# Moving the rows of the normalised input to another place in SBUF

## The chip, the cores and the metric

The kernel runs on one core of a Trainium2 chip. A core has a matrix engine (TensorE, PE in the profile, its weight loads PEld), a vector engine (VectorE, DVE), a scalar engine (ScalarE, ACT), GpSimd (POOL) and SyncE (SP), which issues transfers. On-chip memory (SBUF) has 128 partitions; a tile has a start address in bytes, the same in every partition, and rows of so many bytes. The metric is device time in microseconds for one execution.

## The reference

One layer of a hybrid decoder over 512 tokens with 16 learned meta tokens in front, 1024 channels, float32. What matters here is that one normalised input `u` is multiplied by the many columns of one wide weight matrix:

```python
u = rmsnorm(h, mix_norm_w[i])
proj = u @ w_in[i]                      # (528, 1024) @ (1024, 9248)
u_pool = proj[..., OFF_POOL:OFF_Z]      # all 528 tokens needed
z = proj[..., OFF_Z:OFF_XBC]            # tokens behind the meta tokens
xbc = proj[..., OFF_XBC:OFF_DT]         # all 528
gates = jax.nn.sigmoid(proj[..., OFF_GATE:] + b_gate[i])   # behind the meta tokens
...
y_pool = pool_mixer(u_pool, ...) @ w_pool_up[i]
y_ssd = mamba2_branch(z, xbc, ...) @ w_ssd_out[i]
h = h + (gate_pool * y_pool + gate_ssd * y_ssd) @ w_o[i]
v = rmsnorm(h, mlp_norm_w[i])
h = h + jnp.square(jax.nn.relu(v @ w_ff1[i])) @ w_ff2[i]
out = rmsnorm(h, final_norm_w)          # meta tokens dropped
```

## The kernel before

Every matmul is done in three: a float32 operand is split into a high and a low part of type float32r (ScalarE makes the high part, VectorE the rest), and high by high, high by low and low by high are summed in PSUM. The weights come in blocks of 128 x 1024, loaded by SyncE in the order of use and split into `whi` and `wlo` (lines 68 to 70).

The input lies transposed, channels on the partitions: eight tiles `k` of 128 channels, each with a row of 528 numbers (16 meta tokens, then 512). `xh`, `xl` are the input split, used while the norm is not yet known; `uh`, `ul` (line 119 on) are the normalised input, split. `norm_u` writes them once, about 70 us from the start; all further products with `w_in` read them.

`proj` (line 138 to 141 is its inner step) multiplies one weight block by all eight `k`. For each `k` it issues weights high by `uh[k]`, weights high by `ul[k]`, and weights low by `uh[k]`; the weights are the stationary operand, the rows of `uh`, `ul` the moving one. There are two uses:

- `narrow`: the 512 tokens behind the meta tokens in one matmul: `pz` (in `group_proj`, two blocks to a group), `pgp` and `pgs` (gates).
- `wide`: all tokens in two pieces of 264 columns, or 258 where the first 12 are skipped: `px` (projections to `x`, `B`, `C` of the state space branch) and `pp` (pooling branch).

The work on `uh`, `ul` is woven with that of the state space branch (`ssd`, up to about 510 us): `weave` takes turns between the parts of one group's `ssd` and the projections of the next. After it come the pooling branch with `pool_tile` and `pool_mix` (`pp`, `pg`), `w_pool_up` (`pup`) and the second gates (`pgs`) until 646 us. Then the output projection (`pw`), and the MLP (`pf`, `alpha`, `p2`, `q5`, last the products at line 849). Those do not read `uh`, `ul`; their moving operands are `mh`, `vh`, `vl`, `whi`, `wlo` and the like. `mm3` (lines 86 to 88) issues their three matmuls in the same order as `proj`.

Tiles are laid out by pools: a pool on the left side begins where the pools opened before it end, its tiles one after the other in the order in which they are asked for, each start a multiple of 32 bytes. At address 0 lies a scratch of 16384 bytes for the descriptors of GpSimd's transfers. Of the addresses that the kernel before has:

| tiles | start | modulo 256 |
|---|---|---|
| `raw`, `whi`, `wlo` | 23008 and on, 4096 each | 224 |
| `uh0` to `uh7`, `ul0` to `ul7` | 68064 and on, 2112 each | 224, 32, 96, 160 and again |
| the tokens behind the meta tokens, 64 bytes on | | 32, 96, 160, 224 and again |
| `vh`, `vl`, `mh`, `ml`, `yph`, `ypl`, `yh`, `yl`, `ph`, `pl` | 2048 each | 224 |
| the float32 tiles of `ssd` (pool `gs`), `qhg`, `qlg` among them | 122720 and on | 96 |

The left side of SBUF and the right side meet with little room: in `ssd` the left pools end at 160608 and the right ones begin at 163808; in the pooling branch they end at 128736 and begin at 131040.

Of the kernel before, what the change touches and what calls it, by code (L numbers as in the profile page):

```python
# [9 lines left out]
F32 = mybir.dt.float32  # L10
F32R = mybir.dt.float32r
# [3 lines left out]
P = 128  # L15
D = 1024
SEQ = 512
NM = 16
L = SEQ + NM
HALF = L // 2  # L20
NK = D // P
# [24 lines left out]
def kernel(ctx: ExitStack, tc, xT, x, w, vec, fnw, out):  # L46
    nc = tc.nc
# [68 lines left out]

    u_stack = ExitStack()
    up = u_stack.enter_context(tc.tile_pool(name="up", bufs=1, side="left"))
    uh = [up.tile([P, L], F32R, name=f"uh{k}") for k in range(NK)]
    ul = [up.tile([P, L], F32R, name=f"ul{k}") for k in range(NK)]  # L120

    gc_stack = ExitStack()
    gc = gc_stack.enter_context(tc.tile_pool(name="gc", bufs=2, side="left", reuse_waits="tile"))
# [503 lines left out]
    for half in range(2):  # L627
# [5 lines left out]
        for kk in range(4):  # L633
            wh, wl = block()
            for k2 in range(2):
                k = 2 * kk + k2
# [8 lines left out]
        for kk in range(4):  # L645
            k = 4 * half + kk
# [185 lines left out]
    for t in range(4):  # L832
        T, st = t // 2, slice((t % 2) * P, (t % 2 + 1) * P)
        n = 0
        for half in range(2):
            parts = [(0, 512)] if half == 0 or t < 3 else [(0, 256), (256, 256)]
            for a, m in parts:
# [4 lines left out]
                for k, seg in ((1, (A11, 3)[T]), (0, (A12, A22)[T])):  # L842
                    wh, wl = wq[k, half]
                    for p in range(2):
                        x0 = p * 512 + a
                        f = i == 0 and not (T == 0 and half == 0)
# [151 lines left out]
```

## Time and profile before

| | us |
|---|---|
| median of 3 runs | 1035.13 (1034.96 to 1035.14) |
| the profiled execution | 1035.26 |
| its span, first to last instruction | 1033.5 |

| matmuls by moving operand | columns | count |
|---|---|---|
| `pz`, `pgp`, `pgs` from `uh`, `ul` | 512 | 336, 120, 192 |
| `px` from `uh`, `ul` | 264 | 1008 |
| `px` from `uh`, `ul` | 258 | 336 |
| `pp` from `uh`, `ul` | 264 | 384 |
| all matmul instructions | | 5700 |

A profile is of one execution. It has for every engine the start and the duration of each instruction and what released it. Matmuls overlap: a row's mean duration is longer than the distance from one start to the next, which is the pace of the stream. The span is some 1.8 us shorter than the time of the same execution.

### The profile page before, as it was taken

What the parts mean: (1) busy time and instruction counts of PE and PEld (TensorE: products, weight loads), DVE (VectorE), ACT (ScalarE), POOL (GpSimd) and SP (SyncE); (2) the same over time, 40 slices, a digit from 0 to 9 for tenths busy, and PEclk for the clock granted to TensorE, in tenths of its full rate; (3) what the DMA queues carried; (4) which work ended last, traced back from release to release, by engine and by line L of the source; (5) the groups of instructions that cost most, each with busy time, mean ns of one, the idle gap of its engine ahead of it and who ended that gap; (6) DMA issues with size and microseconds to landing.
All of it is one profiled execution on the core that took longest, in us unless ns stands there. A gap on an engine that the chain in (4) does not pass through costs nothing.

```text
span 1033.5 us, 13995 instructions
## 1 busy us (share of the span) xinstructions
PE 1019.6 (99%) x5700; PEld 880.2 (85%) x5700; DVE 714.2 (69%) x932; ACT 542.3 (52%) x706; POOL 9.9 (1%) x24
## 2 busy tenths in 40 slices
PE   7999999999999999999999999999999999999997
PEld 7889988898879898988998888878888888888886
DVE  7978787687636586878664345645686676776866
ACT  7675968586627349573443123344555354454444
POOL 0100000000000000000000000000000000000000
PEclk9999999999999999999999999999999999999999
DMA  6343041414332321413232323533324323334112
GB/s 229 110 140 103 21 164 37 148 47 137 102 112 73 103 101 41 146 59 111 77 107 95 102 81 102 204 126 122 99 82 123 103 81 122 102 102 123 42 41 82
DMA packets 29424, 106.01 MB, mean 103 GB/s; under 512 B 3312, under 2 KB 4272, under 8 KB 28336
## 3 DMA queue, kind: packets, MB, share of 16 engines
q1 hardware_dynamic: 26640, 93.14, 28.8%
q0 software_dynamic: 2000, 11.08, 2.9%
q8 instruction: 45, 0.74, 0.3%
q10 hardware_dynamic: 720, 0.91, 0.3%
q14 instruction: 19, 0.16, 0.0%
HBM read 102.95 MB, written 2.16 MB: 102 GB/s over the span
## 4 chain that ended last, share of the span: by engine, by line
PE 97%; DVE 1%; DMA 1%; ACT 0%; issue 0%; SPq 0%; ACTq 0%
PE px L138 6%; PE px L141 6%; PE px L139 6%; PE pf L86 6%; PE pf L87 6%; PE pf L88 6%; PE alpha L742 3%; PE alpha L743 3%; PE alpha L744 3%; PE pz L139 3%; PE pz L141 3%; PE pz L138 3%; PE py L416 2%; PE pso L86 2%; PE pp L141 2%; PE pp L139 2%
## 5 line engine op out<-in xcount | busy, mean ns | idle before, releaser
L69 ACT CAST whi<-raw 128x1024 fp32r<-128x1024 f32 (+2 forms) x141 | 145.4, 1037 | 274.3 <-PE pf L87 61.3
L70 DVE TENSOR_TENSOR wlo<-raw,whi 128x1024 fp32r<-128x1024 f32 (+2 forms) x141 | 169.8, 1206 | 151.5 <-ACT whi L69 151.5
L138 PE MATMUL px<-uh,whi 128*128 128x264 f32 (+1 forms) x448 | 121.0, 291 | 0.7 <-DVE ct L280 0.7
L139 PE MATMUL px<-ul,whi 128*128 128x264 f32 (+1 forms) x448 | 118.2, 284 | 0.0
L86 PE MATMUL pf<-vh,whi 128*128 128x512 f32 x256 | 99.7, 389 | 1.2 <-DVE vl L651 1.2
L87 PE MATMUL pf<-vl,whi 128*128 128x512 f32 x256 | 99.6, 389 | 0.0
L88 PE MATMUL pf<-vh,wlo 128*128 128x512 f32 x256 | 99.6, 389 | 0.0
L141 PE MATMUL px<-uh,wlo 128*128 128x264 f32 (+1 forms) x448 | 91.5, 285 | 0.0
L138 PEld LDWEIGHTS px<-uh,whi 128*128 128x128 f32 x448 | 84.6, 189 | 2.8 <-issue 2.6
L139 PEld LDWEIGHTS px<-ul,whi 128*128 128x128 f32 x448 | 84.4, 188 | 0.3
L141 PEld LDWEIGHTS px<-uh,wlo 128*128 128x128 f32 x448 | 69.4, 188 | 0.3 <-issue 0.3
L693 DVE TENSOR_TENSOR slo<-b,shi 128x1024 fp32r<-128x1024 f32 x35 | 42.7, 1220 | 31.6 <-ACT shi L692 31.6
L692 ACT CAST shi<-b 128x1024 fp32r<-128x1024 f32 x35 | 36.7, 1050 | 51.9 <-PE pf L87 36.5
L86 PEld LDWEIGHTS pf<-vh,whi 128*128 128x128 f32 x256 | 48.1, 188 | 11.5 <-DVE vl L651 1.5
L88 PEld LDWEIGHTS pf<-vh,wlo 128*128 128x128 f32 x256 | 48.0, 188 | 10.0
L87 PEld LDWEIGHTS pf<-vl,whi 128*128 128x128 f32 x256 | 48.1, 188 | 9.8
L742 PE MATMUL alpha<-shi,hh 128*128 128x512 f32 x140 | 54.6, 390 | 0.0
L743 PE MATMUL alpha<-slo,hh 128*128 128x512 f32 x140 | 54.5, 389 | 0.0
L744 PE MATMUL alpha<-shi,hl 128*128 128x512 f32 x140 | 54.5, 389 | 0.0
L754 DVE TENSOR_TENSOR ht<-ht,alpha 128x1024 f32<-128x1024 f32 x35 | 42.6, 1216 | 6.1 <-PE alpha L744 6.1
L139 PE MATMUL pz<-ul,whi 128*128 128x512 f32 x112 | 44.3, 395 | 0.0
L141 PE MATMUL pz<-uh,wlo 128*128 128x512 f32 x112 | 44.1, 394 | 0.0
(330 smaller groups left out, 2395.8 us busy)
## 6 DMA issues: line engine op xcount, KB each, us to landing
raw<-in_w SPq DMA_DIRECT2D x137, 512.0 KB, 3.6
b<-in_w SPq DMA_DIRECT2D x28, 512.0 KB, 3.5
abc<-acs_d POOLq DMA_DIRECT2D x8, 1024.0 KB, 7.2
xt<-in_xT SPq DMA_DIRECT2D x8, 264.0 KB, 6.2
ht<-in_x POOLq DMA_DIRECT2D x4, 512.0 KB, 5.0
w<-in_w SPq DMA_DIRECT2D x4, 512.0 KB, 3.5
out_dram<-out SPq DMA_DIRECT2D x4, 320.0 KB, 2.4
raw<-in_w SPq DMA_DIRECT2D x2, 384.0 KB, 5.5
```

What stands on the lines that cost most here:

```text
L69: act.copy(hi[:, c], raw[:, c])
L70: dve.tensor_tensor(lo[:, c], raw[:, c], hi[:, c].bitcast(F32), op=ALU.subtract)
L86: pe.matmul(ps, ah, bh, start=first, stop=False)
L87: pe.matmul(ps, ah, bl, start=False, stop=False)
L88: pe.matmul(ps, al, bh, start=False, stop=last)
L138: pe.matmul(o, wh, rhs[0][k][:, c], start=k == 0, stop=False)
L139: pe.matmul(o, wh, rhs[1][k][:, c], start=False, stop=False)
L141: pe.matmul(o, wl, rhs[0][k][:, c], start=False, stop=k == NK - 1)
L693: dve.tensor_tensor(lo, src, hi.bitcast(F32), op=ALU.subtract)
L742: pe.matmul(ps[t], a[0], wh[:, cs], start=f, stop=False, skip_group_check=True)
L743: pe.matmul(ps[t], a[0], wl[:, cs], start=False, stop=False, skip_group_check=True)
L744: pe.matmul(ps[t], a[1], wh[:, cs], start=False, stop=l, skip_group_check=True)
```

## The change

The rows of `uh` and `ul` become tiles of 576 numbers, 2304 bytes, of which the last 528 are used: `uh[k]` is the part from column 48 on, so that all code that indexes it stays as it is. A tile of 64 bytes, `u_pad`, which nothing reads or writes, is asked for ahead of them. The scratch for the descriptors of GpSimd's transfers is 8192 bytes instead of 16384, and everything on the left side lies that much lower. No instruction is added, taken away or moved in its queue.

```diff
     up = u_stack.enter_context(tc.tile_pool(name="up", bufs=1, side="left"))
-    uh = [up.tile([P, L], F32R, name=f"uh{k}") for k in range(NK)]
-    ul = [up.tile([P, L], F32R, name=f"ul{k}") for k in range(NK)]
+
+    up.tile([P, 16], F32, name="u_pad")
+    uh = [up.tile([P, 64 + SEQ], F32R, name=f"uh{k}")[:, 64 - NM :] for k in range(NK)]
+    ul = [up.tile([P, 64 + SEQ], F32R, name=f"ul{k}")[:, 64 - NM :] for k in range(NK)]
...
-    nc = bacc.Bacc("TRN2", target_bir_lowering=False, num_devices=1)
+    nc = bacc.Bacc("TRN2", target_bir_lowering=False, num_devices=1, dynamic_dma_scratch_size=8192)
```

## The prediction

> **What bounds the kernel now.** I read the page first, for which engine sets the time; then the chain that ended last; then the groups of matmuls with their shapes apart; then the timeline of TensorE at a place where matmuls with different moving operands follow one another; last the busy times of stretches.
>
> ```profile
> span 1033.5 us, 13995 instructions
> PE 1019.6 (99%) x5700; PEld 880.2 (85%) x5700; DVE 714.2 (69%) x932; ACT 542.3 (52%) x706; POOL 9.9 (1%) x24
> ...
> PEclk9999999999999999999999999999999999999999
> ...
> PE 97%; DVE 1%; DMA 1%; ACT 0%; issue 0%; SPq 0%; ACTq 0%
> ```
>
> The chain is TensorE for 97%, at full clock throughout. No other engine's work and no transfer can give more than the few per cent left; what counts is the distance from one matmul's start to the next. The next view, groups by shape, shows that matmuls of one size are not equally long.
>
> ```profile
> L86 PE MATMUL pf<-vh,whi 128*128 128x512 f32 x256 | 99.7, 389 | 1.2 <-DVE vl L651 1.2
> ...
> L138 PE MATMUL px<-uh,whi 128*128 128x264 f32 x336 | 90.7, 290 | 0.7 <-DVE ct L280 0.7
> ...
> L139 PE MATMUL pz<-ul,whi 128*128 128x512 f32 x112 | 44.3, 395 | 0.0
> L141 PE MATMUL pz<-uh,wlo 128*128 128x512 f32 x112 | 44.1, 394 | 0.0
> L138 PE MATMUL pz<-uh,whi 128*128 128x512 f32 x112 | 43.9, 392 | 0.0
> ...
> L87 PE MATMUL pup<-ypl,whi 128*128 128x512 f32 x64 | 24.9, 389 | 0.0
> ```
>
> Both kinds do the same work (128x128 weights, 512 columns, high by high, high by low, low by high). With `uh` and `ul` as moving operand one takes 392 to 395 ns, with `vh`, `ypl` 389. The timeline shows what that means in pace (start, duration):
>
> ```profile
> 554.97 0.39 PE L88 MATMUL pg<-ph,wlo 128*128 128x512 f32 x1
> 555.20 0.40 PE L138 MATMUL pgs<-uh,whi 128*128 128x512 f32 x1
> 555.43 0.40 PE L139 MATMUL pgs<-ul,whi 128*128 128x512 f32 x1
> 555.67 0.39 PE L141 MATMUL pgs<-uh,wlo 128*128 128x512 f32 x1
> ...
> 560.78 0.40 PE L86 MATMUL pup<-yph,whi 128*128 128x512 f32 x1
> 561.01 0.39 PE L87 MATMUL pup<-ypl,whi 128*128 128x512 f32 x1
> 561.24 0.39 PE L88 MATMUL pup<-yph,wlo 128*128 128x512 f32 x1
> 561.47 0.39 PE L86 MATMUL pup<-yph,whi 128*128 128x512 f32 x1
> ```
>
> ```profile
> core 0: us, PE busy (x) PEld busy (x) DVE busy (x) ACT busy (x) POOL busy (x), PEclk, DMA share, GB/s
> 555.20:560.78 5.58, 5.58 (x26) 4.51 (x24) 2.20 (x3) 1.61 (x2) 0.00 (x0) 1.00 0.58 188
> 561.24:566.70 5.46, 5.46 (x26) 4.52 (x25) 1.50 (x2) 1.65 (x3) 0.00 (x0) 1.00 0.33 99
> ```
>
> Both stretches start 24 matmuls of 512 columns (the count adds those that reach in): 5.58/24 = 232.5 ns each for `pgs`, 5.46/24 = 227.5 for `pup`, at one clock. So the dense stream has a settled pace, 227 ns, and the stream from `uh`/`ul` does not reach it. The starts (in ns in the trace) show more. With operands at one place modulo 256 the pace settles after a break: after `px`, the `pso` stream goes 347, 240, 235, 233, 236, 224, 231, 236, 228, 233, 231 and then 226 to 227; `pg` after `pp` 236, 233, then 227. At 555.20 it is the other way: settled at 227, the first three from `uh0`, `ul0`, `uh0` (32 modulo 256) take 237, 235, 232, and the stream stays at 226 to 241 while each k comes from a row 2112 bytes on, which moves the place by 64 (32, 96, 160, 224).
>
> **The change, part by part.**
>
> *Where the rows come to lie.* Before, the first row starts at byte 68064, 224 modulo 256. The scratch gives up 8192 bytes (a multiple of 256), the pad tile takes 64: the row starts at 32, the meta tokens (192 bytes in) at 224, the tokens behind them (64 more) at 32. So by the allocation the tokens lie at 32 and not at 224, if the unused pad gets its room; rows are 2304 = 9 x 256 bytes, so all sixteen agree, and `ul[k]` lies 18432 bytes, again a multiple, behind `uh[k]`.
>
> *Narrow matmuls* (tokens only, 512 columns): `pz` 336, `pgp` 120, `pgs` 192 with `uh`/`ul`, in all 648. Their distances sum to 150.2 us, 231.9 each; all at 227 would be 147.1, so 3.1 us is the most. They come in 7 runs of 48 and 13 of 24. If a constant place lets them settle, each run pays its start: 2 matmuls by `pg`, 10 by `pso`. With 10 left unsettled in 20 runs the gain is 448 x 4.9 = 2.2 us, with 3 it is 588 x 4.9 = 2.9. I take 6: 528 x 4.9 = 2.6. It is all on the path. If a place of 32 does not settle, the nearest rows are those at 32 now: 237, 235, 232 after a settled stretch, 231.6, 233.4, 233.4 within one (k = 4). From 227 to 237 for all 648 is -3.1 to +3.3 us.
>
> *Wide matmuls* (all tokens in two pieces): 1392 of 264 columns (`px`, `pp`) and 336 of 258. They start at 224, 32, 96, 160 and 0, 64, 128, 192 now; afterwards at 224 and 0 for every k. Their median distance is 122 ns at nearly each of the eight places (120 to 125), 120 for 258 columns. I take no change. The bounds: the settled 256-column pieces of the last matmuls (`last`, line 849) pace at 120; with 512 columns at 227 that is 0.418 ns per column, so a settled 264 would be 123.3 and a 258 120.8: +1.3 x 1392 + 0.8 x 336 = +2.1 us. If all 264 came down to 120, -2.0 x 1392 = -2.8.
>
> *Tiles behind the rows* on the left side move by 3136 - 8192, 64 modulo 256. `ph`, `pl` go from 224 to 32: 48 matmuls `pg`, 0 to +10 ns each, at most +0.5 us; I take +0.1. The float32 matmuls do not mind now: `pcb` paces at 112 with weights at 32 and at 96, `ptx` at 109 with data at 32, 96, 160, 224: 0.
>
> *Writing the rows* (`norm_u`, 24 instructions): same counts and sizes, 0 on the path; it ends while TensorE has `ptb`, `ptx` and weights to do. Were they 5% slower, 24 x 0.7 us x 5% = 0.8 us of work on two engines under TensorE's 10 us to `px`.
>
> *Scratch for GpSimd's transfers, halved.* They are 17, with 2000 packets in the whole run; the first `abc` is issued at 49.73 and lands in 7.2 us, and its first reader, `eb`, starts at 71.8. 15 us cover it. If half the room made it land twice as late it would still be in time: 0. `ht` waits for the last `pgs` as before, 217.5 us of waiting that costs nothing. No wait is added, no queue gets an instruction more. Reuse: behind the shorter left side the `gs` tiles end at 155552 instead of 160608 and lie on fewer rows of `xt`, so no wait gets later.
>
> *Sum*: -2.6 + 0 + 0.1 = -2.5 us. The profiled execution took 1035.26, 1.8 beyond its span; 1033.5 - 2.5 + 1.8 = 1032.8; the median of the runs is 0.1 lower: 1032.6.
>
> [...] The rows say that place matters to a stream of matmuls (227 against 232). [...]
>
> **The rivals.**
>
> *Place is not the cause* (chance 0.06). The `uh` streams would be slow for something else, the work around them. For it: they share their stages with busy ScalarE and VectorE. Against: `pgs` and `pup` alternate within 12 us with similar loads, and their paces differ at once. Time 1035.1.
>
> *The tokens at 32 never settle and pace as now* (0.26). For it: no settled stream in the trace lies anywhere but at 224 modulo 256, where the weights lie too; `png`, both operands at 96, paces 229 to 235, but only two at a time. At 232 to 233 for all: 648 x 0.5 = +0.3: 1035.4.
>
> *Slower: 32 is a bad place for good* (0.18). The three `pgs` at 555.20 show 237 right after a settled stretch; if the constant place holds each matmul there, 648 x 5.1 = +3.3 and 48 `pg` x 10 ns = +0.5: 1038.9. It decides from 235.1 ns on, 3.2 above the present mean. Against: within a run the matmuls at 32 take 231.6 to 233.4.
>
> *The pad takes no room* (0.12), the opposite of my arithmetic: the tokens then do lie at 224, nothing behind them moves modulo 256, and the runs settle as `pup` does: -2.9: 1032.2.
>
> **How the numbers follow.** Forecast (place 32, constant, settles as `pso` does at 224): 0.38, at 1032.6, its own range 1030 to 1034.5 by the wide bounds. Below 0.2%, about what a measurement of this kernel can tell from no change, that is under 1033.06: 0.28 of the forecast, 0.10 of the pad case, 0.04 of the never-settling case with a gain in the wide ones, 0.42 together. Above 1037.2: 0.14 of the bad place, 0.04 of the never-settling with a wide loss, 0.02 of the rest, 0.20. Within: 0.38. Range 1030.3 to 1037.8: it leaves out the upper part of the bad place (0.12) and a full wide gain on top of a settled stream (0.06).
>
> **What would show it.** Right: rows `pz`, `pgp`, `pgs` at 389 to 390 ns instead of 392 to 397, a run of 24 in 5.46 to 5.50 us, 48 in 10.95 instead of 11.12; `pup`'s rows as now; TensorE's busy time down by 2 to 3 us, everything else equal. `px`, `pp` at 284 to 291 as now: if they move, the wide term was wrong. `pz` at 395 or more throughout: the bad place. A longer wait of `eb` for `abc`: the scratch. Wrong it goes if settling needs moving operand and weights at one place, or if the wide matmuls, nearly three times as many, settle on another pace than their mixed one.

## The result, and the profile after

| | before | after |
|---|---|---|
| median of 22 runs each, us | 1035.30 | 1033.66 |
| lowest to highest, us | 1034.49 to 1035.89 | 1033.29 to 1034.82 |
| profiled execution, us | 1035.26 | 1033.66 |
| its span, us | 1033.5 | 1031.9 |

The ratio of after to before is 0.9986, with an interval of 0.9979 to 0.9992: about 1.5 us, 0.14%, less. The interval leaves out 1, so there is a gain, but it is under the 0.2% that the prediction took as the least that a measurement can tell, and the time is 1.1 us over the 1032.6 forecast.

From the page of the changed kernel: span, busy time of the engines, the granted clock, and the chain that ended last by engine.

```profile
span 1031.9 us, 13993 instructions
...
PE 1017.8 (99%) x5700; PEld 880.1 (85%) x5700; DVE 714.5 (69%) x932; ACT 542.5 (53%) x706; POOL 10.0 (1%) x24
...
PEclk9999999999999999999999999999999999999999
...
PE 97%; DVE 1%; DMA 1%; ACT 0%; issue 0%; SPq 0%; ACTq 0%
```

The bound is the same, TensorE at full clock. It was busy for 1.8 us less (1019.6 before); the span is 1.6 us shorter. The weight loads (PEld) and all other engines are within 0.3 us of what they were.

Groups of matmuls with shapes kept apart, changed kernel (busy us, mean ns of one; `uh`, `ul` operands now all lie 32 bytes behind a multiple of 256 by the program's allocation, the weights at 224 as before):

```profile
L86 PE MATMUL pf<-vh,whi 128*128 128x512 f32 x256 | 99.7, 389 | 1.2 <-DVE vl L653 1.2
...
L140 PE MATMUL px<-uh,whi 128*128 128x264 f32 x336 | 91.0, 290 | 0.7 <-DVE ct L282 0.7
...
L140 PE MATMUL pz<-uh,whi 128*128 128x512 f32 x112 | 44.0, 393 | 0.0
L141 PE MATMUL pz<-ul,whi 128*128 128x512 f32 x112 | 43.9, 392 | 0.0
L143 PE MATMUL pz<-uh,wlo 128*128 128x512 f32 x112 | 43.7, 390 | 0.0
...
L87 PE MATMUL pup<-ypl,whi 128*128 128x512 f32 x64 | 24.9, 389 | 0.0
```

Two of the three `pz` rows came down, `pz<-ul,whi` from 395 to 392 and `pz<-uh,wlo` from 394 to 390; `pz<-uh,whi` did not (392 to 393), and none is at the 389 of `pf` and `pup`. `px<-uh,whi` stayed at 290. The timeline of TensorE at the same handover as in the prediction, from `pg` to `pgs` (start, duration, us), and then the busy times of two stretches, 24 `pgs` from there and 48 `px` of 264 columns:

```profile
553.73 0.39 PE L88 MATMUL pg<-ph,wlo 128*128 128x512 f32 x1
553.95 0.39 PE L140 MATMUL pgs<-uh,whi 128*128 128x512 f32 x1
554.18 0.39 PE L141 MATMUL pgs<-ul,whi 128*128 128x512 f32 x1
554.41 0.39 PE L143 MATMUL pgs<-uh,wlo 128*128 128x512 f32 x1
554.64 0.39 PE L140 MATMUL pgs<-uh,whi 128*128 128x512 f32 x1
```

```profile
core 0: us, PE busy (x) PEld busy (x) DVE busy (x) ACT busy (x) POOL busy (x), PEclk, DMA share, GB/s
553.95:559.45 5.50, 5.50 (x26) 4.51 (x24) 2.19 (x3) 1.61 (x2) 0.00 (x0) 1.00 0.59 191
425.41:431.38 5.97, 5.97 (x51) 5.97 (x50) 5.42 (x9) 1.13 (x2) 0.53 (x1) 1.00 0.83 291
```

24 `pgs` take 5.50 us where they took 5.58. In ns from start to start they go 231, 226, 229, 232, 226, 229, 232, 226, 229 and so on: a triple that repeats and has a mean of 229.0. The stream does settle, here at once, but on 229 and not on the 227 of `pup`. The stream before had settled too, which the prediction did not see: from the tenth of the `pgs` that begin at 555.20 on it goes 226, 235, 229, 231, 234, 233, 233, 232, 232, 228, 233, 234 and then 226, 235, 229 again. That is a cycle of twelve matmuls, one round of the four places, with a mean of 231.7. The change has put one cycle in place of another.

To find where the 1.6 us lie I summed the distances from each matmul's start to the next one's, by tile (us, one profiled execution of each kernel):

| | before | after | difference |
|---|---|---|---|
| narrow: `pz` | 77.83 | 77.00 | -0.83 |
| narrow: `pgs` | 44.64 | 44.03 | -0.61 |
| narrow: `pgp` | 27.78 | 27.52 | -0.25 |
| wide: `px`, `pp` | 213.94 | 213.97 | +0.03 |
| `pg`, reading the moved `ph`, `pl` | 10.93 | 11.01 | +0.08 |
| `psl`, six at a time among `pgs` | 11.07 | 11.19 | +0.12 |
| `pso` | 45.29 | 45.12 | -0.17 |
| start-up, from `xh`, `xl` | 61.38 | 61.08 | -0.30 |
| all | 1022.24 | 1020.38 | -1.86 |

The narrow matmuls give 1.69 us and nothing else gives much. In the start-up stage TensorE waits for the first `xh` (5.2 us at the longest before, 5.5 after), and ScalarE, which splits it, for transfers (`raw` and `xt`, 3.2 us before, 3.1 after); in the eleven kernels of this document that leave its rows alone it sums to between 60.8 and 63.0 us, one execution each, so its -0.30 is not shown to be an effect of the change.

### The profile page after: what moved, and what is told of

Read it like the earlier page. It is cut to its first block, busy times and chain, and to the rows that moved or that the text cites. A ratio compares the mean times of both kernels' runs of the same rounds, so it can differ in the third digit from the quotient of the medians.

```text
span 1031.9 us, 13993 instructions
## 1 busy us (share of the span) xinstructions
PE 1017.8 (99%) x5700; PEld 880.1 (85%) x5700; DVE 714.5 (69%) x932; ACT 542.5 (53%) x706; POOL 10.0 (1%) x24
## 4 chain that ended last, share of the span: by engine, by line
PE 97%; DVE 1%; DMA 1%; ACT 0%; issue 0%; SPq 0%; ACTq 0%
PE px L140 6%; PE px L141 6%; PE px L143 6%; PE pf L86 6%; PE pf L88 6%; PE pf L87 6%; PE alpha L744 3%; PE alpha L746 3%; PE alpha L745 3%; PE pz L140 3%; PE pz L141 3%; PE pz L143 3%; PE py L418 2%; PE pp L141 2%; PE pso L86 2%; PE pp L140 2%
## 5 line engine op out<-in xcount | busy, mean ns | idle before, releaser
L140 PE MATMUL pz<-uh,whi 128*128 128x512 f32 x112 | 44.0, 393 | 0.0
```

Of the source, the lines that this page charges most:

```text
L140: pe.matmul(o, wh, rhs[0][k][:, c], start=k == 0, stop=False)
```

## The experiments

Each diff is against the changed kernel, but for the scratch alone, which is against the kernel before. "Place" is a start modulo 256; "distance" is the place of the first moving column minus that of the weights, modulo 256.

**Tokens at 224, where the weights are.** The change without its pad. The tiles behind the rows then have the places that they had before.

```diff
-    up.tile([P, 16], F32, name="u_pad")
```

> The changed kernel without the pad tile: the rows begin at 224 modulo 256, the tokens behind the meta tokens lie at 224, and so do the tiles behind the rows, as before the change. Theory (a constant place lets the stream settle, and where it settles hangs on the place): the 648 narrow matmuls from uh, ul settle at 227 ns instead of the 229.3 of the changed kernel, their sum goes from 148.55 to 147.1 to 147.6 us; pg and psl go back to 227 and 229 to 231; wide ones stay at 122; time 1.2 to 1.8 us under the changed kernel, about 1032.1, 3.0 to 3.3 under before. Rival (only constancy counts, the three-step pattern 232, 226, 229 belongs to the order of proj): narrow ones stay at 229.3, time within 0.4 us of the changed kernel. Rival (the smaller scratch brought the gain): as the changed kernel.

Measured: 1030.81 us beside 1035.32 of the kernel before, ratio 0.9955 (0.9943 to 0.9967). First a row of the kernel before, then groups of this one by shape, and the same two stretches:

```profile
L139 PE MATMUL px<-ul,whi 128*128 128x264 f32 x336 | 88.9, 285 | 0.0
```

```profile
L139 PE MATMUL px<-uh,whi 128*128 128x264 f32 x336 | 90.6, 290 | 0.7 <-DVE ct L281 0.7
L140 PE MATMUL px<-ul,whi 128*128 128x264 f32 x336 | 88.5, 284 | 0.0
...
L139 PE MATMUL pz<-uh,whi 128*128 128x512 f32 x112 | 43.6, 390 | 0.0
L140 PE MATMUL pz<-ul,whi 128*128 128x512 f32 x112 | 43.6, 390 | 0.0
L142 PE MATMUL pz<-uh,wlo 128*128 128x512 f32 x112 | 43.6, 389 | 0.0
```

```profile
core 0: us, PE busy (x) PEld busy (x) DVE busy (x) ACT busy (x) POOL busy (x), PEclk, DMA share, GB/s
551.16:556.60 5.44, 5.44 (x26) 4.50 (x24) 2.20 (x3) 1.61 (x2) 0.00 (x0) 1.00 0.63 193
423.26:429.18 5.92, 5.92 (x51) 5.92 (x50) 5.42 (x9) 1.08 (x2) 0.53 (x1) 1.00 0.83 266
```

24 `pgs` in 5.44 us are 226.7 each, the pace of `pup`; after a break the stream goes 236, 229, 232, 231 and then 226 to 227. The narrow sum is 147.24 us, 3.00 under before. The wide sum was expected to stay and is 212.49, 1.45 under before: 48 `px` take 5.92 us, 5.97 in the change. The pad thus costs the change 2.8 us: 1.31 in the narrow matmuls, 1.48 in the wide ones.

**The smaller scratch alone.**

```diff
-    nc = bacc.Bacc("TRN2", target_bir_lowering=False, num_devices=1)
+    nc = bacc.Bacc("TRN2", target_bir_lowering=False, num_devices=1, dynamic_dma_scratch_size=8192)
```

> The kernel before with the scratch for GpSimd's transfers at 8192 bytes and nothing else: all places as before modulo 256. Theory: no change, narrow sum 150.2 us, time within 0.4 us of before; the transfers of abc land in 7 us as before. Rival (the scratch is part of the gain): up to 1.6 us under before.

Measured: 1035.16 us, ratio 1.0000 (0.9991 to 1.0009). The narrow sum is 150.24 as before, the wide one 213.94 as before. The scratch costs nothing, and a shift of everything on the left side by 8192 bytes, a multiple of 256, leaves each row's place modulo 256 and its pace as they were. All of the gain comes from the rows.

**Tokens at 96 and at 160.** A pad of another size, and a second one behind `ul` so that the tiles behind keep their places (numbers for 96; for 160 they are 48 and 16):

```diff
-    up.tile([P, 16], F32, name="u_pad")
+    up.tile([P, 32], F32, name="u_pad")
...
+    up.tile([P, 32], F32, name="u_tail")
```

> The changed kernel with the tokens at 96 modulo 256 for all k (pad 128 bytes; a second pad behind the rows keeps all other tiles where they were modulo 256 before). Theory (each constant place settles, at its own pace): a repeating pattern after at most 10 matmuls of a run, mean between 227 and 233, narrow sum 147.1 to 151; pg as before at 227.7. Rival (32 settled because it is 64 bytes from the weights' place, others need not): no repeating pattern, 231 to 235 ns, time as before or up to 2 us over it.

> The same with the tokens at 160 modulo 256. Theory: a repeating pattern too, mean between 227 and 233; 64 bytes from the weights' place on the other side, so near the 229.3 of place 32 if the distance alone counts. Rival (no settling away from 224 and 32): 231 to 235 ns without a pattern.

Measured: 1035.29 us at 96, ratio 1.0000 (0.9990 to 1.0009), and 1037.27 at 160, ratio 1.0017 (1.0008 to 1.0026). The tokens at 160, groups by shape:

```profile
L141 PE MATMUL pz<-uh,whi 128*128 128x512 f32 x112 | 44.3, 395 | 0.0
L142 PE MATMUL pz<-ul,whi 128*128 128x512 f32 x112 | 44.3, 395 | 0.0
L144 PE MATMUL pz<-uh,wlo 128*128 128x512 f32 x112 | 44.3, 395 | 0.0
...
L142 PE MATMUL px<-ul,whi 128*128 128x264 f32 x336 | 89.6, 287 | 0.0
```

All three `pz` rows are equal now, at 395: settled, at a bad pace. From start to start the stream at 160 goes 233, 233, 234 and so on, or 231 and 236 in turn; at 96 it has two cycles as well, one of them 229, 238. Place 160 is 64 bytes on the other side of the weights, and was expected near 229 if the distance counted alike on both sides; it does not. So one place for all rows is not what pays: the mean is 232.6 at 96 and 233.3 at 160, against 231.9 of the mixture before. At 160 the wide sum is 1.03 us over before too.

**Weights and rows both at 32.** The tokens at 224 as above, and then 64 bytes ahead of the pool of weights, which move everything on the left side, weights, rows, `vh`, `vl`, `ph`, `pl` among them. The tiles on the right side stay at 224: `yph`, `ypl` (the data of `pup`), `yh`, `yl` (of `pso`, `psp`), `mh`, `ml` (the stationary operands of `pw`) and `hh`, `hl` (those of `alpha`).

```diff
+    lp = ctx.enter_context(tc.tile_pool(name="lp", bufs=1, side="left"))
+    lp.tile([P, 16], F32, name="l_pad")
...
-    up.tile([P, 16], F32, name="u_pad")
```

> The kernel with the tokens at 224 (no pad), and a pad of 64 bytes ahead of the weight tiles, so that weights, rows, vh, vl and ph, pl all lie at 32 modulo 256; the tiles on the right side (yh, yl, yph, ypl, mh, ml, hh, hl) stay at 224. Theory (the distance of the moving operand from the stationary one counts, modulo 256): narrow pz, pgp, pgs, pg and pf at 226.7 as with both at 224; pup (moving 224, weights 32, distance 192) at 233, as the tokens at 160 were with weights at 224; pso likewise; alpha and pw (moving 32, stationary 224, distance 64) at 229. Rival (224 is the good place of the moving operand as such): pz, pgp, pgs, pg and pf at 229, pup at 226.7. Time by both 4 to 6 us over the kernel with 224.

Measured: 1035.82 us, ratio 1.0005 (0.9995 to 1.0014). The time is nearly that of before, but its parts are not. First `alpha` in the kernel before, then groups of this one by shape, and then 24 `pgs` and the 24 `pup` behind them:

```profile
L743 PE MATMUL alpha<-slo,hh 128*128 128x512 f32 x140 | 54.5, 389 | 0.0
```

```profile
L88 PE MATMUL pf<-vh,whi 128*128 128x512 f32 x256 | 99.7, 390 | 1.2 <-DVE vl L654 1.2
...
L746 PE MATMUL alpha<-slo,hh 128*128 128x512 f32 x140 | 55.2, 394 | 0.0
...
L141 PE MATMUL pz<-uh,whi 128*128 128x512 f32 x112 | 43.7, 390 | 0.0
...
L88 PE MATMUL pup<-yph,whi 128*128 128x512 f32 x64 | 25.2, 394 | 0.0
L89 PE MATMUL pup<-ypl,whi 128*128 128x512 f32 x64 | 25.2, 394 | 0.0
L90 PE MATMUL pup<-yph,wlo 128*128 128x512 f32 x64 | 25.2, 394 | 0.0
```

```profile
core 0: us, PE busy (x) PEld busy (x) DVE busy (x) ACT busy (x) POOL busy (x), PEclk, DMA share, GB/s
553.42:558.86 5.44, 5.44 (x26) 4.51 (x24) 2.19 (x3) 1.61 (x2) 0.00 (x0) 1.00 0.59 193
558.86:564.46 5.60, 5.60 (x26) 4.50 (x25) 1.23 (x1) 1.63 (x2) 0.00 (x0) 1.00 0.30 97
```

The rows lie at 32, as in the change, and pace at 226.7 instead of 229, because the weights are at 32 as well. `pup`, which nobody touched, has its data still at 224 and its weights at 32 now, and paces at 5.60/24 = 233.3 instead of 226.7. `alpha`, at a distance of 64, shows 229.1 in the same triple as the `pgs` of the change, also at 64. What counts is the distance between moving operand and weights, not a place as such. Against the kernel before, the narrow and wide matmuls win 4.3 us, and `pup` (+1.27), `alpha` (+0.89), `pso` (+0.75), `psp` (+0.61), `pw` (+0.42) and some smaller ones give back 4.6.

The wide matmuls tell the same. Their pieces start at places 224 and 0 here, as in the change, and sum to 212.56 against 213.97: it is the distance, (192, 224) here and (0, 32) there, that differs. With the tokens at 224 it is (192, 224) too, and the sum 212.49.

**`uh` at 224 and `ul` at 96.** Two pads of 128 bytes, one between `uh` and `ul`.

```diff
-    up.tile([P, 16], F32, name="u_pad")
...
+    up.tile([P, 32], F32, name="u_mid")
...
+    up.tile([P, 32], F32, name="u_tail")
```

> The high parts' tokens at 224, the low parts' at 96, constant over k; all other tiles in their places of before modulo 256. Theory (each matmul pays by its own distance from the weights): a triple takes 226.7 + 232.3 + 226.7, mean 228.6, narrow sum 148.1 us. Rival (a change of place inside the triple breaks the settling, as the change from k to k does before): 231 to 233, narrow sum 149.7 to 151.

Measured: 1035.19 us, ratio 0.9999 (0.9990 to 1.0009). Two runs of 24 `pgs` of the same kernel, 8 us apart:

```profile
core 0: us, PE busy (x) PEld busy (x) DVE busy (x) ACT busy (x) POOL busy (x), PEclk, DMA share, GB/s
547.47:553.07 5.60, 5.60 (x27) 4.51 (x26) 3.23 (x4) 2.20 (x4) 0.00 (x0) 1.00 0.26 94
555.81:561.30 5.49, 5.49 (x25) 4.50 (x24) 2.20 (x3) 1.61 (x2) 0.00 (x0) 1.00 0.54 191
```

The first goes 236, 234, 230 in a cycle, the second 227, 234, 226. Same operands, same distances, two paces: which one a run falls into goes with what stands ahead of it. Seven runs of `pgs` follow `pg`, `pup` or `psl`, whose distance is 0, and pace at 228.9. One of `pgs`, all five of `pgp` and three of `pz` follow `px` or `pp` and pace at 233.3 to 233.6. The other four of `pz` follow `png` and take a third way, at 230.8 to 231.1. That a matmul has a price by its own distance, so that a triple takes the 228.6 expected, comes near only in the first seven runs; in the other thirteen all three matmuls lose the pace.

**Distances 32, 16 and 224.** Three more places of the tokens, to see whether the pace rises with the distance, or with the 32-byte step, or alike on both sides of 0. For place 0 the pads are 8 and 56 numbers, for 192 they are 56 and 8, as above; place 240 goes by longer rows:

```diff
-    up.tile([P, 16], F32, name="u_pad")
-    uh = [up.tile([P, 64 + SEQ], F32R, name=f"uh{k}")[:, 64 - NM :] for k in range(NK)]
-    ul = [up.tile([P, 64 + SEQ], F32R, name=f"ul{k}")[:, 64 - NM :] for k in range(NK)]
+    uh = [up.tile([P, 640], F32R, name=f"uh{k}")[:, 52 : 52 + L] for k in range(NK)]
+    ul = [up.tile([P, 640], F32R, name=f"ul{k}")[:, 52 : 52 + L] for k in range(NK)]
```

> Tokens at 0 modulo 256 (32 bytes past the weights' place; other tiles as before). Theory (the pace rises with the distance past the weights: 226.7 at 0, 229.0 at 64, 232.3 at 128): about 228, settled in a repeating pattern, narrow sum 147.5 to 148.2 us. Rival (a row that begins on a multiple of 256 needs fewer pieces, so it is the best place): under 226, narrow sum under 146.8.

> Tokens of uh, ul at 240 modulo 256, 16 bytes past the weights' place (rows of 2560 bytes; all other tiles as before). Theory (only the full distance of 0 modulo 256 gives 226.8, and what other distances cost follows no simple order): 229 to 234 ns, narrow sum 148.4 to 151.6 us. Rival (the unit that counts is 32 bytes or more, so 16 bytes past is as good as 0): 226.7 to 227.5, narrow sum under 147.6.

> Tokens at 192 modulo 256, 32 bytes ahead of the weights' place (distance 224). Theory (distances off 0 cost 2 to 7 ns, the sign does not matter much): as 32 bytes past it, about 233 ns, narrow sum 150.5 to 151.5 us, time 0.5 to 1.5 us over before. Rival (only moving operands past the weights' place lose, those ahead of it do not): 227 to 228, narrow sum under 148.

Measured: 1036.11 us at 0, ratio 1.0008 (0.9999 to 1.0017); 1034.32 at 240, ratio 0.9990 (0.9981 to 1.0000); 1036.67 at 192, ratio 1.0012 (1.0002 to 1.0021). A place at a multiple of 256 paces at 233.2, so a plain alignment is not what is wanted, and 16 or 32 bytes off the weights is worse than 64. For place 0 both expectations fell, a pace of 228 that rises with the distance and one under 226. All places together, mean from start to start over the 648 narrow matmuls, with the cycle that the runs settle into:

| tokens at | distance | narrow, ns | cycle, ns | distances of wide pieces of 264 | wide sum, us |
|---|---|---|---|---|---|
| 224 | 0 | 227.2 | 226 to 227 | 192, 224 | 212.49 |
| 240 | 16 | 231.6 | 235, 230, 227, 234 | 208, 240 | 213.20 |
| 0 | 32 | 233.2 | 235, 233, 234, 230 | 224, 0 | 213.66 |
| 32 (the change) | 64 | 229.2 | 232, 226, 229 | 0, 32 | 213.97 |
| 96 | 128 | 232.6 | 229, 238 or one of seven | 64, 96 | 213.40 |
| 160 | 192 | 233.3 | 233, 233, 234 or 231, 236 | 128, 160 | 214.97 |
| 192 | 224 | 233.4 | 232, 235 | 160, 192 | 214.17 |
| mixed (before) | 64, 128, 192, 0 | 231.9 | one of twelve | mixed | 213.94 |

Each of these seven constant distances settles into some cycle, and so does the mixture. Only 0 is clearly good (227.2), 64 half as good (229.2), and all others pace at about the mixture's 231.9 or worse (231.6 to 233.4). The differences of the two sums from before give the measured differences of these kernels to within 0.4 us (at 160, +0.95 and +1.03 against 1.95).

The wide sum takes in 336 pieces of 258 columns, which begin 48 and 24 bytes further on than those of 264 (with the tokens at 224, at distances of 240 and 248). For 264 columns alone it is another table than for 512: the 1392 of them take least, 171.3 us, at (192, 224), where 512 columns pace at 233, and most, 173.3, at (128, 160).

**The start-up rows too.** The tokens at 224, and `xh`, `xl` of the start-up stage made alike.

```diff
-    up.tile([P, 16], F32, name="u_pad")
...
-    xh = [pre.tile([P, L], F32R, name=f"xh{k}") for k in range(NK)]
-    xl = [pre.tile([P, L], F32R, name=f"xl{k}") for k in range(NK)]
+    xh = [pre.tile([P, 64 + SEQ], F32R, name=f"xh{k}")[:, 64 - NM :] for k in range(NK)]
+    xl = [pre.tile([P, 64 + SEQ], F32R, name=f"xl{k}")[:, 64 - NM :] for k in range(NK)]
+    pre.tile([P, 32], F32, name="x_pad")
```

> The kernel with the tokens of uh, ul at 224, and xh, xl, the rows used before the norm is known, likewise of 2304 bytes with their tokens at 224. Theory (the same gain for the same kind of row): the 72 pgp matmuls from xh, xl go from 231.8 to 227 to 228, the 48 of pz lose up to 5 ns each where they do not wait, 0.4 to 0.7 us together; time 1030.2 to 1030.5, against 1030.8 with 224 for uh, ul alone. Rival (that stage waits for the splits of weights and input, so a quicker stream only waits longer): time as with uh, ul alone, within 0.2 us.

Measured: 1029.89 us, ratio 0.9949 (0.9937 to 0.9962), the fastest of all. First the group of the kernel before, then those of this one:

```profile
L139 PE MATMUL pgp<-xl,whi 128*128 128x512 f32 x24 | 9.5, 396 | 0.0
```

```profile
L142 PE MATMUL pgp<-xh,wlo 128*128 128x512 f32 x24 | 9.4, 390 | 0.0
L139 PE MATMUL pgp<-xh,whi 128*128 128x512 f32 x24 | 9.3, 389 | 0.0
L140 PE MATMUL pgp<-xl,whi 128*128 128x512 f32 x24 | 9.3, 389 | 0.0
```

These 72 matmuls go from 16.69 to 16.33 us, 231.8 to 226.8 each, as a distance of 0 says. The rest of the start-up waits for other things (its 48 `pz` sum to 11.60 against 11.58). The intervals of this kernel and of the one with `uh`, `ul` alone at 224 overlap; that it is better than that one rests on the 0.36 us of these rows.

## Why the prediction was right or wrong

- **What bounds the kernel.** Right. TensorE stayed 97% of the chain, and the gain is in the distance between matmuls of the rows that moved.
- **Where the rows lie.** Right. By the arithmetic of the allocation `uh0` begins at 68064 - 8192 + 64 = 59936 and all tokens lie at 32; the run without the pad measures 2.85 us less, so the pad takes its room. The rival by which it takes none has the mechanism of that run, and its price was too low: -2.9 was taken, -4.5 measured, since it left the wide matmuls out.
- **Narrow matmuls.** The direction was right and the term was mis-sized: -2.6 was taken, -1.69 measured. The step that failed is "a constant place lets them settle", with the pace that 227 stands for. The streams before were settled as well, on their cycle of twelve at 231.7, so constancy is not what the gain comes from: at 96, 160, 192 and 0 the place is as constant and the pace no better. The change's runs settle faster than taken (within 3 matmuls behind `px`, 5 behind `png`, where 6 were taken), but at 229.0: the rows that served as model, `pso` and `pg`, have their weights at their own place, a distance of 0, and the change makes the distance 64. The last sentence of the prediction names just this as what would make it wrong, and the sum went without it. That there was a gain at all is luck of the distance: of the seven constant ones only 0 and 64 clearly beat the mixture. 648 x (231.9 - 229.2) = 1.75 is the measured gain within its rounding. Of the signs named, `pz` came to 390 to 393 and not to 389 to 390, and TensorE's busy time fell by 1.8 us, not by 2 to 3.
- **Wide matmuls.** 0 was taken, +0.03 measured. But the reason given, the same median at nearly each place, does not carry: other constant places moved them by -1.45 to +1.03 us. Mixed streams hide what a constant distance does, as they did for the narrow ones. That nothing showed is luck of (0, 32). The places given for the pieces are those of 264 columns; the 336 of 258 begin 48 and 24 bytes further on.
- **`pg`.** +0.1 was taken, +0.08 measured. It lies at a distance of 64 now and paces at 229.4. Not foreseen was the handover: `psl`, six matmuls at a distance of 0 between runs at 64, goes 234, 231, 233, 236, 224, 231, and lost 0.12 us; `pup` behind `pgs` lost 0.04.
- **Float32 tiles, `norm_u`, scratch.** 0 each, as taken. `norm_u` begins at 50.2 us and `px` from `uh` at 69.7 as before, `eb` starts at 71.8 as before, and the smaller scratch alone measures 1.0000.
- **Place not the cause; never settling.** Both fell: the same instructions at seven constant places range from 227.2 to 233.4 ns, and the change's runs settle, at 229.0. For the second it was said that no settled stream lies anywhere but at 224; the mixture's cycle of twelve is one.
- **A bad place for good.** Not at 32, but it exists: 160 measures 2.0 us over before. Its price of 237 is never reached; the worst settled pace is 233.4. The 237 that it drew on is the first matmul of a stream behind another one.
- **That place matters to a stream.** Right: the runs show 226.7 ns at best and up to 233.4 for the same work, by the distance of two addresses alone.

What stays open is the mechanism. Why 64 bytes are better than 16, 32 or 128 (229.2 ns against 231.6, 233.2 and 232.6), and why 264 columns prefer distances that 512 do not (171.3 us at (192, 224), where 512 columns take 233.3 and 233.4 ns), no run explains.

## What to carry to other kernels

Where a dense stream of matmuls bounds a kernel, compare the start-to-start pace of groups that do the same work; if one is some per cent slower at the same clock (here 231.9 ns against 226.7), look at the addresses of its moving operand and its weights modulo 256. For 512 columns of this type put both at the same place and keep it so from matmul to matmul (226.7 ns here); a constant distance other than 0 can be worse than a mixture (233.3 ns at 192 against 231.9), and moving the weights instead moved the price to other streams that read them (4.3 us won, 4.6 given back). A pace seen at one distance is no estimate for another (229.0 at 64, 233.2 at 32): take it only from a row with the same distance and the same number of columns.

## What the runs showed of the hardware that was not expected

- The pace of 512-column matmuls, one weight load to each, depends on the distance of moving operand and weights modulo 256: 226.7 ns settled at 0, 229.0 at 64, 231.6 to 233.4 at 16, 32, 128, 192 and 224. Rows that lie 2304 bytes apart, nine times 256, pace alike (226.7 for all eight `k` with the tokens at 224).
- At a constant distance the starts fall into a short cycle that repeats to the nanosecond or two (232, 226, 229 at 64). Four distances in turn (before) settle too, on a cycle of twelve with a mean of 231.7. With two distances in turn, one kernel had three paces for the same instructions, 229, 231 and 233 ns in the mean, by what stood ahead of the run.
- For 264 columns other distances are good than for 512: 1392 matmuls take 171.3 us with their two pieces at (192, 224) and 173.3 at (128, 160).
